# A convolution on rows moved by DMA instead of on transposed features, in a hybrid mixer trunk

## The chip, the cores and the metric

The kernel runs on one core of one Trainium2 chip. The metric is the device time of one launch in microseconds. Of several runs the median counts.

## The reference

One layer of a decoder trunk over 256 tokens of width 2048, in float32: a norm, two causal token mixers fed by one input projection (a gated DeltaNet with 16 heads of 128, and a causal pooling mixer), merged by sigmoid gates and an output projection with a residual; then a gated MLP of width 5632 with a causal depthwise convolution, a residual, and a last norm. What matters here is the path of q, k and v:

```python
proj = jnp.einsum('bsd,de->bse', h, w_in[l])
q, k, v, z, b_raw, a_raw, p_in, g_a, g_b = jnp.split(proj, splits, axis=-1)
qkv = jax.nn.silu(causal_dwconv(jnp.concatenate([q, k, v], axis=-1), conv_qkv_w[l]))
...
def causal_dwconv(x, w):            # width 4 here
    xp = jnp.pad(x, ((0, 0), (width - 1, 0), (0, 0)))
    y = xp[:, 0:seq] * w[0]
    for j in range(1, width):
        y = y + xp[:, j:j + seq] * w[j]
```

Each feature has four taps of its own, and token s sees tokens s−3 to s. After the convolution and silu, q and k are normalised, and the gated delta rule mixes the tokens of each head.

## The kernel before, in words

**Groups.** The mixers run in four groups of four heads (512 features). The loop (L687) does for each group the gemms K, Q, V, P, GB, a short one for the pooling weights, Z and GA. After the four groups come w_out, the MLP's up and down projections and the last norm.

**Weights.** All weights stream in tiles of 512 KB (128 partitions x 1024 float32). For each, `weights()` has a DMA on SyncE's queue fill `raw` (4 buffers), ScalarE rounds it to `whi` (L111), and VectorE forms the remainder `wlo` (L118); `whi` and `wlo` have 3 buffers each, and are made two tiles ahead. In `gemm_a` (L137) a weight tile feeds twelve matmuls: `whi` with the high and the low half of the activations (L148, L149) and `wlo` with the high half (L150). A gemm is eight tiles. Its result stands in PSUM (`psm`, 2 buffers) with tokens on partitions.

**What runs between the matmuls.** At the second tile of a gemm the list `later` is emptied: there the convolution of the gemm before is put. After each weight tile `side()` does one step of `gdn`, the delta rule of the current group, which is a generator: decays (L482 to L511), products of k and q (L518, L520) with their norms, the blocks for a triangular solve sent through DRAM (`cdd`, `lb`, L552 to L556), the solve on VectorE (L563 to L567), its result through DRAM again (`tbd`, `tct`), then `vt`, and from L598 on a chain of small matmuls. `gdn` is started at the second tile of V's gemm. A scheduler places the instructions on the engines' queues within these dependencies; each queue then runs in its order.

**The convolution.** `evict` (L445) copies a gemm's result, scaled by the row norm, from PSUM to `ev` (one buffer, tokens on partitions: 128 x 2 halves x 512 features). `conv_silu` (L452) turns it with eight 128x128 transposes on TensorE (`turned`, L193) so that features lie on partitions and tokens along the row; there a tap is one number per partition, and a shift by s tokens is an offset in the row. Per 128 features ScalarE does the last tap (L463) and VectorE the other three (L466), on `cy` (2 buffers); tanh (L469) and one more VectorE operation (L470) make the silu. For k and q the result with features on partitions is what the delta rule needs. v is needed with tokens on partitions: `gdn` turns it back with eight more transposes (L580) and ScalarE scales it into `vt` (L582).

**The short copies on ScalarE's queue.** All loads that are not weights, `x` or the blocks of the solve go there: norm weights in 16 rows of 512 B (twice), the bias of the MLP's convolution in 44 rows of 512 B (`vrows`), the taps in 96 rows of two times 512 B (`cqrows`) and 66 rows of two times 512 B (`cfrows`), `gwb` in 128 rows of 512 B, `alb` and `dtb` in 128 rows of 64 B each, `psb` four times in 128 rows of 2 KB, later `xt` in 256 rows of 8 KB and `nfin` in 128 rows of 8 KB.

Of the kernel before, what the change touches and what calls it, by code (L numbers as in the profile page):

```python
# [7 lines left out]
F32 = mybir.dt.float32  # L8
F32R = mybir.dt.float32r
I32 = mybir.dt.int32  # L10
AF = mybir.ActivationFunctionType
ALU = mybir.AluOpType

P = 128
S = 256
D = 2048
NH = 16
KD = D // P
# [6 lines left out]
C_Q, C_K, C_V, C_Z = 0, 2048, 4096, 6144  # L25
# [8 lines left out]
def kernel(  # L34
# [20 lines left out]
    nc = tc.nc  # L55
# [11 lines left out]
    def nm(s):  # L67
        cnt[0] += 1
        return f"{s}_{cnt[0]}"

    def pg(shape=(P, 512)):
        return psg.tile(list(shape), F32, tag="g", name=nm("psg"))
# [25 lines left out]
    def weights():  # L98

        begin(taken[0] + AHEAD + 1)  # L100
        taken[0] += 1
        return made[taken[0] - 1]
# [19 lines left out]
    side_work = [iter(())]  # L122

    def side():
        next(side_work[0], None)
# [5 lines left out]
    def pm():  # L131
        return psm.tile([P, 2, 512], F32, tag="m", name=nm("psm"))


    later = []

    def gemm_a(lh, ll, nk):  # L137

        ps = pm()
        for c in range(nk // 2):  # L140
            if c == 1:
                while later:
                    later.pop(0)()
            hi, lo = weights()
            for kk in range(2):
                k = 2 * c + kk
                for t in range(2):
                    mm(ps[:, t, :], lh(k, t), hi[:, kk, :], start=(k == 0), stop=False)  # L148
                    mm(ps[:, t, :], ll(k, t), hi[:, kk, :], start=False, stop=False)  # L149
                    mm(ps[:, t, :], lh(k, t), lo[:, kk, :], start=False, stop=(k == nk - 1))  # L150
                side()
        return ps
# [47 lines left out]
    ident = cpool.tile([P, P], F32, name="ident")  # L200
# [5 lines left out]
    def mtile(i, shape, dt, name):  # L206
        return big.tile(shape, dt, tag=f"m{i}", name=name)

    mix = tc.tile_pool(name="mix", bufs=1)
    mp = mix.__enter__()  # L210
# [17 lines left out]
    for k2 in range(KD // 2):  # L228
# [6 lines left out]
        for kk in range(2):  # L235
# [3 lines left out]
                                           op0=ALU.mult, op1=ALU.subtract)  # L239
# [74 lines left out]
    rs1 = rstd_rows(ssq, None)  # L314
    rsh = cpool.tile([P, 2], F32, name="rsh")
# [110 lines left out]
    for g, win in enumerate(WINDOWS):  # L426
# [3 lines left out]
        for cs in (slice(0, P + PAD), slice(P + PAD, NB)):  # L430
            b = bd[:, cs]
            n = cs.stop - cs.start
# [9 lines left out]
    mhi = []  # L442
    mlo = []

    def evict(ps):  # L445

        e = mp.tile([P, 2, 512], F32, tag="ev", bufs=1, name=nm("ev"))
        for t in range(2):
            nc.scalar.activation(e[:, t, :], ps[:, t, :], AF.Copy, scale=rs1[:, t : t + 1])
        return e  # L450

    def conv_silu(e, kind, g, dst):  # L452

        pts = turned(e)
        y = mp.tile([P, 4, S], F32, tag="cy", bufs=2, name=nm("cy"))
        for f in range(4):
            r = kind * 16 + 4 * g + f
            gs = pts[f // 2][:, f % 2, :]

            def w(j):  # L460
                return cqw[:, j * 48 + r : j * 48 + r + 1]

            nc.scalar.activation(y[:, f, :], gs, AF.Copy, scale=w(3))  # L463
            for j in (2, 1, 0):
                s = 3 - j
                nc.vector.scalar_tensor_tensor(y[:, f, s:], gs[:, : S - s], w(j), y[:, f, s:],  # L466
                                               op0=ALU.mult, op1=ALU.add)
        th = mp.tile([P, 4, S], F32, tag="th", name=nm("th"))
        nc.scalar.activation(th, y, AF.Tanh)  # L469
        nc.vector.scalar_tensor_tensor(dst, th, 1.0, y, op0=ALU.add, op1=ALU.mult)  # L470

    def gdn(g, kq, vT, res):

        ga0 = mp.tile([P, 4, 512], F32, tag="ga0", name=nm("ga0"))
        ga1 = mp.tile([P, 4, 256], F32, tag="ga1", name=nm("ga1"))
        vt = mp.tile([P, 2, 4, P], F32, tag="vt", name=nm("vt"))
        ssk = mp.tile([P, 2, 4], F32, tag="ssk", name=nm("ssk"))
        nk = mp.tile([P, 2, 4], F32, tag="nk", name=nm("nk"))
# [33 lines left out]
        for hp in range(2):  # L512
# [3 lines left out]
            for h in (h0, h0 + 1):  # L516
# [5 lines left out]
                for t, src in ((0, pg0[:, 0:P]), (1, pg1[:, 0, :])):  # L522
                    nc.vector.tensor_tensor_reduce(jk, src, ident, scale=1.0, scalar=0.0, op0=ALU.mult,
                                                   op1=ALU.add, accum_out=ssk[:, t, h : h + 1])
# [6 lines left out]
            for h in (h0, h0 + 1):  # L531
# [4 lines left out]
                                               op0=ALU.mult, op1=ALU.mult)  # L536
# [3 lines left out]
                                               op0=ALU.mult, op1=ALU.mult)  # L540
# [34 lines left out]

        for h in range(4):
            yield
            pvt = pg([P, 2, P])
            for t in range(2):
                nc.tensor.transpose(pvt[:, t, :], vT[:, h, t * P : (t + 1) * P], ident)  # L580
            for t in range(2):
                nc.scalar.activation(vt[:, t, h, :], pvt[:, t, :], AF.Copy, scale=nk[:, t, h : h + 1])  # L582
        for _ in range(WAIT - 3):
            yield
        tcm = mp.tile([P, 8, B0], F32, tag="r1h", name=nm("tcm"))
# [100 lines left out]

    for g in range(4):  # L687
        kq = mp.tile([P, 4, 2, S], F32, tag="kq", bufs=1, name=nm("kq"))
        vT = mp.tile([P, 4, S], F32, tag="vT", bufs=1, name=nm("vT"))
        for kind, dst in ((1, kq[:, :, 0, :]), (0, kq[:, :, 1, :]), (2, vT)):  # L690
            if kind == 2:
                res = []
                later.append(lambda g=g, kq=kq, vT=vT, res=res: side_work.__setitem__(0, gdn(g, kq, vT, res)))
            ps = ps_k0 if kind == 1 and g == 0 else gemm_a(xh, xl, KD)
            e = evict(ps)
            later.append(lambda e=e, kind=kind, g=g, dst=dst: conv_silu(e, kind, g, dst))


        win = WINDOWS[g]
        psb = scales(g)  # L700
        ps = gemm_a(xh, xl, KD)
        e = evict(ps)
        phi = mtile(g, [P, 4, S], F32R, nm("phi"))
        plo = mtile(4 + g, [P, 4, S], F32R, nm("plo"))

        def pooled(e=e, g=g, phi=phi, plo=plo):
            for f2 in range(2):
                pt = pg([P, 2, S])
                for ff in range(2):
                    fs = slice((2 * f2 + ff) * P, (2 * f2 + ff + 1) * P)  # L710
                    mm(pt[:, ff, P:S], e[:, 1, fs], bands[:, g, P + PAD : NB], start=True, stop=False,
                       skip_group_check=True)
                    mm(pt[:, ff, 0 : P + PAD], e[:, 0, fs], bands[:, g, 0 : P + PAD], start=False, stop=True,
                       skip_group_check=True)
                fs = slice(2 * f2, 2 * f2 + 2)
                nc.scalar.copy(phi[:, fs, :], pt)
                nc.vector.tensor_tensor(plo[:, fs, :], pt, phi[:, fs, :].bitcast(F32), op=ALU.subtract)

        later.append(pooled)

        def gate(ps, tag):
            th = mp.tile([P, 2, 512], F32, tag=tag, name=nm("gate"))
            for t in range(2):
                nc.scalar.activation(th[:, t, :], ps[:, t, :], AF.Tanh, scale=rsh[:, t : t + 1])
            return th

        tb = gate(gemm_a(xh, xl, KD), "th")
        ps = gemm_a(lambda k, t: phi[:, k, t * P : (t + 1) * P], lambda k, t: plo[:, k, t * P : (t + 1) * P], 4)
        yb = mp.tile([P, 2, 512], F32, tag="yb", name=nm("yb"))
        nc.vector.tensor_tensor(yb, ps, psb.unsqueeze(1).to_broadcast([P, 2, 512]), op=ALU.mult)  # L730
        nc.vector.scalar_tensor_tensor(yb, tb, 1.0, yb, op0=ALU.add, op1=ALU.mult)

        ps = gemm_a(xh, xl, KD)
        sz = mp.tile([P, 2, 512], F32, tag="sz", name=nm("sz"))
        nc.vector.scalar_tensor_tensor(sz, gate(ps, "th"), 1.0, ps, op0=ALU.add, op1=ALU.mult)
        ta = gate(gemm_a(xh, xl, KD), "th")
        nc.vector.scalar_tensor_tensor(sz, ta, 1.0, sz, op0=ALU.add, op1=ALU.mult)
        sz4 = sz.rearrange("p t (h d) -> p (t h) d", h=4)
        nc.vector.tensor_tensor(sz4, sz4, gwb.unsqueeze(1).to_broadcast([P, 8, P]), op=ALU.mult)
        drain()  # L740
        nc.vector.tensor_tensor(sz, res[0].rearrange("p t h d -> p t (h d)"), sz, op=ALU.mult)
        nc.vector.tensor_tensor(sz, sz, yb, op=ALU.add)
        mh = mtile(g, [P, 4, S], F32R, f"mhi{g}")
        ml = mtile(4 + g, [P, 4, S], F32R, f"mlo{g}")
        mhi.append(mh)
        mlo.append(ml)

        def mixed(sz=sz, mh=mh, ml=ml):
            for f2, pt in enumerate(turned(sz)):
                fs = slice(2 * f2, 2 * f2 + 2)  # L750
                nc.scalar.copy(mh[:, fs, :], pt)
                nc.vector.tensor_tensor(ml[:, fs, :], pt, mh[:, fs, :].bitcast(F32), op=ALU.subtract)

        later.append(mixed)
# [14 lines left out]
    for c in range(4):  # L769
        ps = gemm_a(at(mhi), at(mlo), KD)  # L770
# [5 lines left out]
        for k2 in range(2):  # L776
# [5 lines left out]
            for kk in range(2):  # L782
# [4 lines left out]
                                               op0=ALU.mult, op1=ALU.subtract)  # L787
# [9 lines left out]
    for c in range(DFF // 512):  # L797
        ps = gemm_b(lambda k: fhl[:, k], KD)
# [13 lines left out]
        ps = gemm_b(lambda k: fhl[:, k], KD)  # L812
# [15 lines left out]
    for c in range(2):  # L828
        ps = pm()
# [18 lines left out]
    for t in range(2):  # L848
# [14 lines left out]
        for c in (0, 2, 1, 3):  # L863
            xs = xt[:, t, c * 512 : (c + 1) * 512]
            if c < 2:
                nc.vector.scalar_tensor_tensor(xs, xs, rs, nfin[:, c * 512 : (c + 1) * 512],
                                               op0=ALU.mult, op1=ALU.mult)
# [34 lines left out]
```

## Time and profile before

| | |
|---|---|
| median of 3 runs | 1593.93 us (1593.29 to 1594.85) |
| the profiled execution | 1594.1 us, span 1592.3 us |
| TensorE busy | 1568.1 us, 98% |
| VectorE busy | 1066.7 us, 67% |
| ScalarE busy | 750.1 us, 47% |
| GpSimd busy | 115.7 us, 7% |
| DMA | 291.62 MB, 183 GB/s over the span |

In the profile PE is TensorE's matmul side, PEld its weight loads, DVE VectorE, ACT ScalarE, POOL GpSimd, SP SyncE. A group's row reads: line, engine, operation, output <- inputs, shapes, count | busy time, mean ns of one | idle time of the engine just before, and what ended most of it. A matmul's own time there (0.39 us) is longer than the pace at which matmuls follow each other, because they overlap. In the chain of waits a row is start, length, what; in the timeline it is start, length, engine, line, operation, with the idle time before it in brackets. A row of the issues view gives queue, count, KB of each and the median time from issue to landing. Line numbers in the text are those of the kernel before, except where the new code is meant.

### The profile page before, as it was taken

The numbers are of one execution on the slowest core, as the hardware profiler recorded it, in microseconds if no ns is written. First come the engines' busy times: TensorE is split into PE (matmuls) and PEld (weight loads), VectorE is DVE, ScalarE is ACT, GpSimd is POOL, SyncE is SP. The second block draws the span as 40 slices with busy tenths as digits, with TensorE's granted clock in tenths as the row PEclk, the third lists the DMA queues.
The fourth block names the chain that finished last, engine by engine and source line by source line (L and its number), as shares of the span: only waits on it lengthen the run. The fifth ranks groups of instructions, "written<-read, shape, count | busy, mean of one in ns | idle before, by whom it ended". The sixth has DMA issues, their size and how long they took to land.

```text
span 1592.3 us, 21435 instructions
## 1 busy us (share of the span) xinstructions
PE 1568.1 (98%) x8116; PEld 1317.5 (83%) x8116; DVE 1066.7 (67%) x1624; ACT 750.1 (47%) x969; POOL 115.7 (7%) x132
## 2 busy tenths in 40 slices
PE   8999999999999999999999999999999999999997
PEld 6878888888888888887788888888888888888886
DVE  6778758786778757786555777666666677444445
ACT  6455435544455445544454544444444444333334
POOL 3020100110020100102000000000000000000000
PEclk9999999999999999999999999999999999999999
DMA  7656656566556656665556666666666666656563
GB/s 251 185 153 191 193 144 179 168 189 176 159 152 189 198 145 177 170 191 162 200 184 182 187 187 192 190 186 187 185 195 186 187 191 209 201 191 197 191 193 132
DMA packets 159789, 291.62 MB, mean 183 GB/s; under 512 B 17974, under 2 KB 21062, under 8 KB 159302
## 3 DMA queue, kind: packets, MB, share of 16 engines
q1 hardware_dynamic: 157792, 285.77, 60.8%
q10 hardware_dynamic: 1894, 4.48, 0.8%
q8 instruction: 63, 1.03, 0.3%
q14 instruction: 40, 0.33, 0.1%
HBM read 287.07 MB, written 3.15 MB: 182 GB/s over the span
## 4 chain that ended last, share of the span: by engine, by line
PE 89%; DVE 3%; DMA 3%; issue 3%; POOL 2%; SPq 1%; ACT 0%; DVEq 0%; POOLq 0%
PE psm L150 12%; PE psm L149 12%; PE psm L148 12%; PE psm L172 10%; PE psg L172 10%; PE psg L173 5%; PE psm L173 5%; PE psg L836 3%; PE psg L838 3%; PE psg L837 3%; PE psm L838 2%; PE psm L836 2%; PE psm L837 2%; DVE wlo L118 1%; PE psg L518 1%
## 5 line engine op out<-in xcount | busy, mean ns | idle before, releaser
L118 DVE TENSOR_TENSOR wlo<-raw,whi 128x1024 fp32r<-128x1024 f32 x528 | 657.8, 1247 | 414.1 <-ACT whi L111 407.8
L111 ACT CAST whi<-raw 128x1024 fp32r<-128x1024 f32 x530 | 557.8, 1053 | 753.7 <-PE psm L149 331.4
L150 PE MATMUL psm<-wlo,xhl 128*128 128x512 f32 x896 | 352.9, 394 | 2.7 <-DVE wlo L118 2.7
L148 PE MATMUL psm<-whi,xhl 128*128 128x512 f32 x896 | 352.1, 393 | 1.9 <-ACT xhl L237 1.9
L149 PE MATMUL psm<-whi,xhl 128*128 128x512 f32 x896 | 351.9, 393 | 0.0
L172 PE MATMUL psm<-fhl,whi 128*128 128x512 f32 x704 | 245.9, 396 | 0.0
L172 PE MATMUL psg<-fhl,whi 128*128 128x512 f32 x704 | 237.8, 394 | 0.0
L150 PEld LDWEIGHTS psm<-wlo,xhl 128*128 128x128 f32 x896 | 168.6, 188 | 38.4 <-DVE wlo L118 4.3
L148 PEld LDWEIGHTS psm<-whi,xhl 128*128 128x128 f32 x896 | 168.7, 188 | 35.9 <-ACT xhl L237 2.3
L149 PEld LDWEIGHTS psm<-whi,xhl 128*128 128x128 f32 x896 | 168.6, 188 | 34.7
L173 PE MATMUL psm<-fhl,wlo 128*128 128x256 f32 x704 | 194.2, 279 | 0.0
L173 PE MATMUL psg<-fhl,wlo 128*128 128x256 f32 x704 | 178.6, 279 | 0.0
L172 PEld LDWEIGHTS psm<-fhl,whi 128*128 128x128 f32 x704 | 131.3, 188 | 30.4
L172 PEld LDWEIGHTS psg<-fhl,whi 128*128 128x128 f32 x704 | 129.2, 188 | 24.0
L173 PEld LDWEIGHTS psg<-fhl,wlo 128*128 128x128 f32 x704 | 132.4, 188 | 6.9
L173 PEld LDWEIGHTS psm<-fhl,wlo 128*128 128x128 f32 x704 | 132.5, 188 | 1.1
L836 PE MATMUL psg<-whi,hhi 128*128 128x512 f32 x176 | 68.6, 390 | 0.0
L836 PE MATMUL psm<-whi,hhi 128*128 128x512 f32 x176 | 68.5, 389 | 0.0
L837 PE MATMUL psm<-whi,hlo 128*128 128x512 f32 x176 | 68.5, 389 | 0.0
L837 PE MATMUL psg<-whi,hlo 128*128 128x512 f32 x176 | 68.5, 389 | 0.0
L838 PE MATMUL psm<-wlo,hhi 128*128 128x512 f32 x176 | 68.5, 389 | 0.0
L838 PE MATMUL psg<-wlo,hhi 128*128 128x512 f32 x176 | 61.7, 389 | 0.0
(233 smaller groups left out, 1515.3 us busy)
## 6 DMA issues: line engine op xcount, KB each, us to landing
raw<-in_w_in_dram SPq DMA_DIRECT2D x226, 512.0 KB, 3.8
raw<-in_w_up_dram SPq DMA_DIRECT2D x176, 512.0 KB, 3.9
raw<-in_w_down_dram SPq DMA_DIRECT2D x88, 512.0 KB, 3.9
raw<-in_w_out_dram SPq DMA_DIRECT2D x32, 512.0 KB, 3.6
raw<-in_pool_w_dram SPq DMA_DIRECT2D x8, 512.0 KB, 3.9
x<-in_x_dram SPq DMA_DIRECT2D x4, 512.0 KB, 8.5
lb<-cdd SPq DMA_DIRECT2D x16, 128.0 KB, 2.7
xt<-in_x_dram ACTq DMA_DIRECT2D x1, 2048.0 KB, 8.3
```

Source lines behind the costliest of these rows:

```text
L111: nc.scalar.copy(hi, raw)
L118: nc.vector.tensor_tensor(lo, raw, hi.bitcast(F32), op=ALU.subtract)
L148: mm(ps[:, t, :], lh(k, t), hi[:, kk, :], start=(k == 0), stop=False)
L149: mm(ps[:, t, :], ll(k, t), hi[:, kk, :], start=False, stop=False)
L150: mm(ps[:, t, :], lh(k, t), lo[:, kk, :], start=False, stop=(k == nk - 1))
L172: mm(ps[f], hi[:, kk, fs], rhl(k), start=(k == 0), stop=False, skip_group_check=True)
L173: mm(ps[f][:, 1, :], lo[:, kk, fs], rhl(k)[:, 0, :], start=False, stop=(k == nk - 1), skip_group_check=True)
L518: mm(pg0, kq[:, h, 0, 0:P], kq[:, h, :, :], start=True, stop=True)
L836: mm(acc[c][t], lh(k, t), hi[:, kk, :], start=(k == 0), stop=False)
L837: mm(acc[c][t], ll(k, t), hi[:, kk, :], start=False, stop=False)
L838: mm(acc[c][t], lh(k, t), lo[:, kk, :], start=False, stop=(k == KF - 1))
```

## The change

For v, `conv_silu` is no longer called. V's gemm is evicted with half the row norm (`rsh`). Then, on tokens:

- Three tiles get copies of `ev` moved on by one, two and three tokens. For a move by j, rows 0 to 127−j of `ev` (each 4 KB, both token halves side by side) go to rows j to 127; the last j rows of the first half (2 KB each) go to the first j rows of the second half; GpSimd clears the first j rows of the first half. The copies are issued from ScalarE's queue. The first two tiles use the two buffers of `cy`, the third has one of its own.
- The four taps, 512 numbers each, are loaded over all 128 partitions by four copies of 256 KB on SyncE's queue, into the buffers of `sz` and `yb`.
- Four products and three sums of 128x1024 on VectorE, tanh on ScalarE and one VectorE operation give v with tokens on partitions. `vt` is scaled from it directly; the transposes at L580 are gone.

The copies are issued right behind the eviction; the arithmetic goes on the list `later`, at the second tile of P's gemm. In the new order of VectorE's queue the product on the first move stands behind `wlo` of P's third weight tile, ahead of the end of Q's convolution and of `wlo` of P's fourth tile; in the first group ahead of `wlo` of P's fourth tile too, behind part of the side work.

```diff
-    def evict(ps):
+    def evict(ps, by=None):
+        by = rs1 if by is None else by
         e = mp.tile([P, 2, 512], F32, tag="ev", bufs=1, name=nm("ev"))
         for t in range(2):
-            nc.scalar.activation(e[:, t, :], ps[:, t, :], AF.Copy, scale=rs1[:, t : t + 1])
+            nc.scalar.activation(e[:, t, :], ps[:, t, :], AF.Copy, scale=by[:, t : t + 1])
         return e
+
+    def later_tokens(e, g):
+        moved = []
+        for j in (1, 2, 3):
+            m = mp.tile([P, 2, 512], F32, name=nm("mv"), **(dict(tag="cy", bufs=2) if j < 3 else dict(tag="mv")))
+            nc.gpsimd.memset(m[0:j, 0, :], 0.0)
+            nc.scalar.dma_start(m[j:P], e[0 : P - j])
+            nc.scalar.dma_start(m[0:j, 1, :], e[P - j : P, 0, :])
+            moved.append(m)
+        taps = []
+        for n, tag in enumerate(("sz", "yb")):
+            tp = mp.tile([P, 2, 512], F32, tag=tag, name=nm("taps"))
+            for i in range(2):
+                nc.sync.dma_start(tp[:, i, :], conv_qkv_w[0, 2 * n + i, C_V + 512 * g : C_V + 512 * g + 512]
+                                  .partition_broadcast(P))
+                taps.append(tp[:, i, :].unsqueeze(1).to_broadcast([P, 2, 512]))
+        return moved, taps
+
+    def conv_tokens(e, moved, taps):
+        m1, m2, m3 = moved
+        for m, j in ((m1, 2), (m2, 1)):
+            nc.vector.tensor_tensor(m, m, taps[j], op=ALU.mult)
+        nc.vector.tensor_tensor(m1, m1, m2, op=ALU.add)
+        for m, j in ((e, 3), (m3, 0)):
+            nc.vector.tensor_tensor(m, m, taps[j], op=ALU.mult)
+            nc.vector.tensor_tensor(m1, m1, m, op=ALU.add)
+        th = mp.tile([P, 2, 512], F32, tag="th", name=nm("th"))
+        nc.scalar.activation(th, m1, AF.Tanh)
+        nc.vector.scalar_tensor_tensor(m1, th, 1.0, m1, op0=ALU.add, op1=ALU.mult)
+        return m1
...
-    def gdn(g, kq, vT, res):
+    def gdn(g, kq, vals, res):
...
-            pvt = pg([P, 2, P])
             for t in range(2):
-                nc.tensor.transpose(pvt[:, t, :], vT[:, h, t * P : (t + 1) * P], ident)
-            for t in range(2):
-                nc.scalar.activation(vt[:, t, h, :], pvt[:, t, :], AF.Copy, scale=nk[:, t, h : h + 1])
+                nc.scalar.activation(vt[:, t, h, :], vals[0][:, t, h * P : (h + 1) * P], AF.Copy,
+                                     scale=nk[:, t, h : h + 1])
...
-        vT = mp.tile([P, 4, S], F32, tag="vT", bufs=1, name=nm("vT"))
-        for kind, dst in ((1, kq[:, :, 0, :]), (0, kq[:, :, 1, :]), (2, vT)):
-            if kind == 2:
-                res = []
-                later.append(lambda g=g, kq=kq, vT=vT, res=res: side_work.__setitem__(0, gdn(g, kq, vT, res)))
+        for kind, dst in ((1, kq[:, :, 0, :]), (0, kq[:, :, 1, :])):
             ps = ps_k0 if kind == 1 and g == 0 else gemm_a(xh, xl, KD)
             e = evict(ps)
             later.append(lambda e=e, kind=kind, g=g, dst=dst: conv_silu(e, kind, g, dst))
+        res = []
+        vals = []
+        later.append(lambda g=g, kq=kq, vals=vals, res=res: side_work.__setitem__(0, gdn(g, kq, vals, res)))
+        e = evict(gemm_a(xh, xl, KD), rsh)
+        mt = later_tokens(e, g)
+        later.append(lambda e=e, mt=mt, vals=vals: vals.append(conv_tokens(e, *mt)))
```

## The prediction

> **What bounds the kernel now.** I read the page first (engines, queues, chain, groups), then the windows, the forms of each line, the issues, and the timeline around the first group's V and P gemms.
>
> ```profile
> span 1592.3 us, 21435 instructions
> ...
> PE 1568.1 (98%) x8116; PEld 1317.5 (83%) x8116; DVE 1066.7 (67%) x1624; ACT 750.1 (47%) x969; POOL 115.7 (7%) x132
> ...
> q1 hardware_dynamic: 157792, 285.77, 60.8%
> q10 hardware_dynamic: 1894, 4.48, 0.8%
> ...
> PE 89%; DVE 3%; DMA 3%; issue 3%; POOL 2%; SPq 1%; ACT 0%; DVEq 0%; POOLq 0%
> ...
> L118 DVE TENSOR_TENSOR wlo<-raw,whi 128x1024 fp32r<-128x1024 f32 x528 | 657.8, 1247 | 414.1 <-ACT whi L111 407.8
> ...
> L150 PE MATMUL psm<-wlo,xhl 128*128 128x512 f32 x896 | 352.9, 394 | 2.7 <-DVE wlo L118 2.7
> ```
>
> TensorE is busy 98% of the span and carries 89% of the chain. The kernel is bound by its matmuls: a TensorE instruction removed is a gain of its own length, and anything added elsewhere costs only what it makes TensorE wait. The one way by which VectorE reaches TensorE is `wlo`: a weight tile's twelve matmuls need it, and over 896 matmuls they waited 2.7 us in all. The whole execution took 1594.1 us, 1.8 us more than its span and 0.2 us above the median of the three runs (1593.93), so sums against it and against the median are the same within their error.
>
> How long can VectorE be held up before TensorE notices? Before, it is held up once per group by the copy that fills `lb`. VectorE's timeline in group 0, then TensorE's:
>
> ```profile
> 127.84 0.42 DVE L565 TENSOR_TENSOR tmp<-lb,tb 128x248 f32<-128x248 f32 x1 [3.86 <-DMA lb<-cdd]
> ...
> 128.95 1.22 DVE L118 TENSOR_TENSOR wlo<-raw,whi 128x1024 fp32r<-128x1024 f32 x1
> ```
> ```profile
> 130.22 0.50 PE L150 MATMUL psm<-wlo,xhl 128*128 128x512 f32 x1 [0.93 <-DVE wlo L118]
> ```
>
> A hold of 3.86 us cost TensorE 0.93 us: a stall of a few microseconds is hidden by the `wlo` tiles made ahead (three buffers), and beyond that each microsecond is passed on in full.
>
> **The change part by part.** Prices first, from the view of groups by form:
>
> ```profile
> L466 DVE SCALAR_TENSOR_TENSOR cy<-psg,cqw,cy 128x254 f32<-128x254 f32 x48 | 21.3, 472 | 0.0
> ...
> L449 ACT ACTIVATE ev<-psm,rs 128x512 f32<-128x512 f32 x32 | 20.2, 681 | 1.6 <-PE psm L150 1.6
> L813 DVE TENSOR_TENSOR gs<-gs,y 128x1024 f32<-128x1024 f32 x11 | 13.5, 1226 | 1.1
> L193 PE MATMUL psg<-ident,ev 128*128 128x128 f32 x96 | 12.8, 272 | 0.0
> ```
> ```profile
> 67.55 0.92 PE psg L193 x8
> ```
>
> *Transposes removed.* Eight of v at L193 and eight back at L580 per group, 64 in all. In the chain eight take 0.92 us, so 64 × 0.115 = 7.4 us come off TensorE. That is the whole gain.
>
> *Arithmetic swapped.* Per group VectorE loses 12 operations at 0.47 (5.7 us) and gets seven of 128x1024 at 1.23 (8.6 us): 3 us more on an engine at 67%, free by itself. ScalarE loses four copies at L463, the `vt` copies only read elsewhere; GpSimd gets three memsets of one to three rows (7% busy). All at nothing.
>
> *The moves.* Six copies per group are issued from ScalarE's queue: 127, 126 and 125 rows of 4 KB moved on by one, two and three tokens, and three wraps of one to three rows. No row shows an SBUF-to-SBUF copy or one of 127 rows, so its price must be bounded. How copies are divided over the 16 engines can be read off this queue, q10:
>
> ```profile
> raw<-in_w_in_dram SPq DMA_DIRECT2D x226, 512.0 KB, 3.8
> ...
> xt<-in_x_dram ACTq DMA_DIRECT2D x1, 2048.0 KB, 8.3
> ...
> cfrows<-in_conv_ffn_w_dram ACTq DMA_DIRECT2D x1, 66.0 KB
> ...
> vrows<-in_conv_ffn_b_dram ACTq DMA_DIRECT2D x1, 22.0 KB
> ...
> dtb<-in_dt_bias_dram ACTq DMA_DIRECT2D x1, 8.0 KB
> ```
>
> Fourteen copies go through it, between `xt` and `dtb` in that list. By their shapes in the code they have 1680 rows: 528 of 512 B, 256 of 64 B, 512 of 2 KB, 384 of 8 KB. The queue counts 1894 packets, 214 more. One closing packet per engine used would be 14 × 16 = 224 if every copy ran on all 16; ten are missing. Only two copies have row counts that 16 doesn't divide: `vrows` of the bias with 44 rows, `cfrows` with 66. If each ran on 11 engines (44 = 11 × 4, 66 = 11 × 6), the sum is 12 × 16 + 22 = 214, exactly. Had they been cut into blocks of rows rounded up, they would use 15 and 14, and three would be missing. So a copy uses the largest number of engines up to 16 that divides its rows. 127 is prime: the first move runs on one engine; 126 rows run on 14; 125 on 5. The Trainium skill, page "DMA: Bandwidth & Descriptors", section "Why a DMA increments its semaphore by 16 and not by 1", states this division and names 127 partitions as a case that gets one engine; no run of before shows that case.
>
> What one engine moves, from the busiest stretch of the windows view (columns: length, busy of PE, PEld, DVE, ACT, POOL, clock, DMA share, GB/s):
>
> ```profile
> 12.00:18.00 6.00, 6.00 (x24) 5.02 (x23) 5.76 (x13) 5.57 (x15) 0.00 (x0) 1.00 0.88 318
> ```
>
> 318 / (0.88 × 16) = 22.6 GB/s per engine, so 127 × 4096 B = 0.520 MB take 23.0 us. By q1's row (60.8% of 16 engines for 1592.3 us over 285.77 MB = 54.2 us per MB) they take 28.2. I take 23.0, a queue full of packets being nearer to that stretch, and allow 18 to 29. The skill's page just named, section "Specifications", gives some 27 GiB/s per engine, which would make an estimate of 18 us and a sum 20 us lower.
>
> *When the move is late.* Let E be the end of group g's V gemm. The eviction takes 2 × 0.68 = 1.4 us, then ScalarE has two small exponentials and the wrap's issue: the long move is issued near E + 2.4. A raw tile lands 3.8 us after issue although its 32 KB per engine take 1.45 at 22.6 GB/s, so some 2.35 us come on top; and the same engine carries its sixteenth of what else flies: 1 MB of taps (2.9 us) and one or two raw tiles (1.45 each), much of it before, so 2 (0 to 6). Landing: E + 2.4 + 23.0 + 2.35 + 2 = E + 29.8. In the changed kernel's order VectorE has the product on the first move (L475) right behind `wlo` of P's third weight tile, and waits there. Queued behind it are the last operation of Q's convolution (L503), then `wlo` of P's fourth tile: 3 × 1.2 = 3.6 us, so that tile is ready at E + 33.4. TensorE has three tiles and two matmuls of the fourth, 38 × 0.23 = 8.7 us (its pace is in the rows below), and nothing else: the side work waits for Q's convolution too. Stall: 33.4 − 8.7 = **24.7 us per group**. The cover of a few microseconds is in that number already.
>
> The second move reuses the buffer that L503 frees, so it is issued after the first has landed: 9 rows per engine (1.6 us) + 2.35 against some 3.6 us of VectorE work on what lies between; I take 1 us per group (0 to 2). The third, 125 rows on five engines, lies behind the first on the shared engine (25 rows, 4.5 us) and VectorE reaches it 4.8 us later: nothing. Moves: 4 × 25.7 = **103 us**, with ends 4 × 18 = 72 (transfer 18, no shared traffic, nothing for the second move) and 4 × 36 = 144 (transfer 29, traffic 6, second move 2).
>
> *The clock after a stall.* The chain in the start-up, after a first idle time:
>
> ```profile
> 12.82 0.43 PE psm L149
> ...
> 14.81 0.23 PE psm L148
> ```
>
> TensorE's matmuls took 0.43 us at 12.8 and 0.23 at 14.8; a stretch of some 4 us at half pace would cost 2 us. I put that behind each long stall: 4 × 2 = 8 (0 to 10).
>
> *The tail of the mixers.* The heads' side work starts some seven weight tiles later, so the last group's closes inside w_out, whose first two tiles then hold weight buffers. Waits of that kind are there already:
>
> ```profile
> 773.16 0.50 PE L148 MATMUL psm<-whi,mhi 128*128 128x512 f32 x1 [0.91 <-ACT whi L111]
> ...
> 774.42 0.50 PE L150 MATMUL psm<-wlo,mhi 128*128 128x512 f32 x1 [0.53 <-DVE wlo L118]
> ```
>
> One tile costs 1.4 us; four more such, half covered by side matmuls, +3 (0 to 8). *Taps:* four 256 KB copies per group on SyncE's queue, 4 MB over the kernel at a DMA share of 0.6: hidden, except 0.5 us in the start-up, where they stand ahead of raw tiles.
>
> **Sum**: 1594.1 − 7.4 + 103 + 8 + 3 + 0.5 = **1701 us**. Its own range: 1594 − 7 + 72 + 0 = 1659 to 1594 − 7 + 144 + 10 + 8 = 1749.
>
> **The rivals.**
> *The moves are spread over all engines, and still late.* Against: the 214 packets. For: no 127-row copy is shown. Then a move costs what a raw tile does, 3.8 us, + 2 of shared traffic, and lands at E + 8.2; `wlo` at E + 11.8 against 8.7 and 1 for the second move give 4 us of stall per group, with the tail 1594 − 7 + 16 + 3 = 1606.
> *Spread and hidden: the change is faster.* The point that decides is E + 8.7 − 3.6 = E + 5.1: a first move that lands by then costs nothing. With the issue straight behind the eviction (E + 1.4) and 3.8 us it lands at E + 5.2. Then only transposes and tail count: 1594 − 7 + 3 = 1590, at best 1587.
> *One engine, slower still.* Reading and writing SBUF through one engine might cost both ways (46 us), or raw tiles take half of it: + 23 us per group, 1701 + 92 = 1793. For: no row shows SBUF to SBUF. Against: raw tiles stop flowing once TensorE stalls.
>
> **How the numbers follow.** One engine at the price above 0.83; spread and late 0.06; spread and hidden 0.05; slower still 0.06. What a measurement tells from no change is about 0.2%, 3.2 us. Faster: 0.04, most of the hidden case. Same: 0.03, the rest of it and the mildest of the late one. Slower: 0.93. The range runs from 1640 (the low end, less 5 us per group for an engine quicker still) to 1749 and leaves out all three rivals and little else, some 0.2.
>
> **What would show it.** Right: in the waits, VectorE at L475 on the copy from `ev` four times at some 20 us or more; the issues view gives the long move 25 to 31 us to land, the 126-row one a few; TensorE's wait for `wlo` of L118 at L150 grows from 2.7 to about 100 us, in four pieces, each behind a V gemm, with matmuls at 0.43 us behind each; L193 drops from 96 to 64 transposes of `ev`, L580 is gone. Wrong: a long move that lands within 6 us; a VectorE wait at L475 without a stall of TensorE; or a time under 1610.

## The result, and the profile after

The changed kernel takes 1677.39 us in the median of its runs (1677.33 to 1681.23) against 1593.93; the ratio is 1.0528, with an interval of 1.0516 to 1.0540. It is slower by 83 us, where 1701 was forecast, with a range of 1640 to 1749. The profiled execution is the longest of the runs: its span is 1679.1 us, 86.8 more than before.

The page of the changed kernel:

```profile
span 1679.1 us, 21338 instructions
...
PE 1578.3 (94%) x8052; PEld 1318.2 (79%) x8052; DVE 1079.4 (64%) x1604; ACT 746.0 (44%) x953; POOL 125.6 (7%) x144
...
q10 hardware_dynamic: 3654, 10.72, 1.8%
...
L148 PE MATMUL psm<-whi,xhl 128*128 128x512 f32 x896 | 355.7, 397 | 40.3 <-ACT whi L111 38.6
L150 PE MATMUL psm<-wlo,xhl 128*128 128x512 f32 x896 | 355.1, 396 | 12.6 <-DVE wlo L118 12.6
...
L475 DVE TENSOR_TENSOR mv<-mv,taps 128x1024 f32<-128x1024 f32 x8 | 9.8, 1225 | 93.9 <-DMA mv<-ev 71.6
```

TensorE is busy 10.2 us longer and idle 76.6 us longer (100.8 against 24.2). VectorE stands idle 93.9 us ahead of the products at L475. Its waits and TensorE's (waited for: total, times, longest):

```profile
PE psm L148 <- ACT whi L111: 40.9, 7, 10.4
PE psg L551 <- DVE kq L503: 26.3, 3, 9.0
PE psm L150 <- DVE wlo L118: 13.1, 8, 9.1
```

So TensorE waits on two things, and the first is ScalarE's cast, not `wlo`. The timeline of group 1 shows why (V's gemm ends near 293.0). ScalarE and its queue first, then TensorE, then VectorE:

```profile
295.94 10.01 ACTq L459 DMA_DIRECT2D mv<-ev  x1
306.28 3.44 ACTq L460 DMA_DIRECT2D mv<-ev  x1
309.77 1.06 ACT L502 ACTIVATE th<-cy 128x1024 f32<-128x1024 f32 x1 [13.46 <-issue]
310.73 1.98 ACT L111 CAST whi<-raw 128x1024 fp32r<-128x1024 f32 x2
```
```profile
311.81 0.79 PE L148 MATMUL psm<-whi,xhl 128*128 128x512 f32 x1 [9.58 <-ACT whi L111]
322.07 2.08 PE L551 MATMUL psg<-kq 128*128 128x512 f32 x2 [9.04 <-DVE kq L503]
```
```profile
319.65 1.23 DVE L475 TENSOR_TENSOR mv<-mv,taps 128x1024 f32<-128x1024 f32 x1 [22.31 <-DMA mv<-ev]
320.79 1.22 DVE L503 SCALAR_TENSOR_TENSOR kq<-th,cy 128x1024 f32<-128x1024 f32 x1
```

The long move was issued at 295.2 (0.66 us). The next issue, of the third move, takes ScalarE's queue 10.0 us, its wrap 3.4 more, and the casts behind them come at 310.7. Meanwhile VectorE waits for the long move until 319.65, 24.4 us after its issue (24.4 to 25.5 in the four groups). TensorE's two gaps, 9.6 and 9.0 us, are one stall with few matmuls in it; in the four groups the stall is 17.6 to 19.2 us, 74 in all.

What the DMA engines did in that time, first the windows view (length, busy of PE, PEld, DVE, ACT, POOL, clock, DMA share, GB/s), then the queues in the same window (packets, MB, share of 16 engines):

```profile
314.00:322.00 8.00, 0.00 (x0) 0.00 (x0) 2.35 (x3) 0.00 (x0) 0.00 (x0) 0.50 0.06 27
```
```profile
q10 hardware_dynamic: 53, 0.21, 6.5%
```

One engine of 16 is 6.25%. For eight microseconds it alone works, at 27 GB/s, and the fifteen others stand idle with everything else.

### The profile page after: what moved, and what is told of

Same layout as the page of the kernel before. It is cut to its first block, busy times and chain, and to the rows that moved or that the text cites. A ratio compares the mean times of both kernels' runs of the same rounds, so it can differ in the third digit from the quotient of the medians.

```text
span 1679.1 us, 21338 instructions
## 1 busy us (share of the span) xinstructions
PE 1578.3 (94%) x8052; PEld 1318.2 (79%) x8052; DVE 1079.4 (64%) x1604; ACT 746.0 (44%) x953; POOL 125.6 (7%) x144
## 4 chain that ended last, share of the span: by engine, by line
PE 54%; DMA 2%; POOL 1%; DVE 0%; issue 0%; ACT 0%; SPq 0%; DVEq 0%; POOLq 0%
PE psm L172 10%; PE psg L172 10%; PE psg L173 5%; PE psm L173 5%; PE psm L150 3%; PE psm L148 3%; PE psm L149 3%; PE psg L869 2%; PE psg L871 2%; PE psg L870 2%; PE psm L870 2%; PE psm L871 2%; PE psm L869 2%; DMA mv<-ev 1%; PE psg L551 0%
## 5 line engine op out<-in xcount | busy, mean ns | idle before, releaser
L148 PE MATMUL psm<-whi,xhl 128*128 128x512 f32 x896 | 355.7, 397 | 40.3 <-ACT whi L111 38.6
L150 PE MATMUL psm<-wlo,xhl 128*128 128x512 f32 x896 | 355.1, 396 | 12.6 <-DVE wlo L118 12.6
L475 DVE TENSOR_TENSOR mv<-mv,taps 128x1024 f32<-128x1024 f32 x8 | 9.8, 1225 | 93.9 <-DMA mv<-ev 71.6
```

Source lines behind the costliest of these rows:

```text
L475: nc.vector.tensor_tensor(m, m, taps[j], op=ALU.mult)
```

## The experiments

**The division of rows.** The first run cuts every move at 112 rows, which 16 divides.

```diff
-            nc.scalar.dma_start(m[j:P], e[0 : P - j])
+            nc.scalar.dma_start(m[j : j + 112], e[0:112])
+            nc.scalar.dma_start(m[j + 112 : P], e[112 : P - j])
```

> Each move is cut into two copies: its first 112 rows (16 x 7) and the remaining 15, 14 or 13; nothing else is changed, and the order on VectorE's queue around the products stays the one of the changed kernel. Theory (the 127 rows of the first move lie on one engine, 127 x 0.16 us of packets): the first move lands some 4 us after its issue instead of 24, the issue of the third move no longer takes 10 us of ScalarE, the stall behind each V gemm falls from 19 us to 1 to 3, and the time to 1594 - 7 + 8 + 7 (tail as in the changed kernel) + 1 = about 1603 us (1596 to 1608). Rival 1 (copies from SBUF to SBUF are slow by themselves, or these 1.5 MB collide with the weight tiles): the bytes are the same, so the landing stays over 12 us and the time over 1640. Rival 2 (it is the longer arithmetic on VectorE that starves TensorE): no change, 1675.

Measured: 1603.08 us, ratio to before 1.0054 (1.0039 to 1.0069). The same bytes, two copies for one, and 74 us are gone. VectorE's wait for the moves and TensorE's for `wlo` in that run:

```profile
DVE mv L476 <- DMA mv<-ev: 22.5, 7, 5.2
...
PE psm L150 <- DVE wlo L118: 9.9, 9, 3.2
```

The wait at the product falls from 22 to 24 us to 5 at most, and the stalls behind the V gemms to 1.2 to 3.7 us per group, where 1 to 3 were expected. Copies from SBUF to SBUF are not slow by themselves, and the longer arithmetic starves nobody.

**No moves at all.** The products read `ev` in place of the moved tiles:

```diff
-            nc.vector.tensor_tensor(m, m, taps[j], op=ALU.mult)
+            nc.vector.tensor_tensor(m, e, taps[j], op=ALU.mult)
```

> Leaves the moves out: the three tiles are written by the products straight from ev, without the copies and the clearing of their first rows; taps, seven VectorE operations, tanh and the rest stay. Theory: what is left is the removed transposes (-7.4 us), the taps, the arithmetic and the later tail: 1588 to 1596, no wait of VectorE for a copy of ev, no stall of TensorE over 1 us behind a V gemm. Rival 2 (arithmetic on VectorE starves TensorE): stalls behind the V gemms of some microseconds remain and the time is over 1600.

Measured: 1589.06 us, ratio 0.9967 (0.9954 to 0.9980). This is what the rest of the change is worth: some 5 us faster. From one V eviction to the next the groups take 182.0 us in the mean against 184.8 before; behind the last V, up to the MLP, 208.0 against 204.7, so the later closing part takes some of it back.

**A ladder of row counts.** The second and third moves are cut as above; the first differs from group to group.

```diff
+            cut = (P - j, 122, 124, 112)[g] if j == 1 else 112
+            nc.scalar.dma_start(m[j : j + cut], e[0:cut])
```

> A ladder in one kernel. The second and third moves are cut at 112 rows as in the spread version; the first move has one copy of 127 rows in group 0, 122 + 5 rows in group 1, 124 + 3 in group 2 and 112 + 15 in group 3. If a copy uses the largest number of engines up to 16 that divides its rows, these are 1, 2, 4 and 16 engines with 127, 61, 31 and 7 rows of 4 KB each, at 0.16 us a row 20, 10, 5 and 1 us. VectorE's waits at the product on the first move then come down in steps of 10, 5 and 4 us from one group to the next, and TensorE's stalls are near 18, 8, 3 and 1 us: some 30 us in all, 1624 us. Rival (the third move's issue, which holds ScalarE's queue for 10 us, is the cause): since that one is cut here, group 0 already shows a stall under 10 us. Rival (a copy of over 112 rows runs on all 16 engines, cut by bytes): no steps between the groups.

Measured: 1640.06 us in one run. VectorE's timeline at the product on the first move, groups 0 to 3 (127, 122, 124, 112 rows):

```profile
117.80 1.23 DVE L478 TENSOR_TENSOR mv<-mv,taps 128x1024 f32<-128x1024 f32 x1 [23.11 <-DMA mv<-ev]
...
313.04 1.23 DVE L478 TENSOR_TENSOR mv<-mv,taps 128x1024 f32<-128x1024 f32 x1 [11.96 <-DMA mv<-ev]
...
505.38 1.22 DVE L478 TENSOR_TENSOR mv<-mv,taps 128x1024 f32<-128x1024 f32 x1 [10.08 <-DMA mv<-ev]
...
690.33 1.23 DVE L478 TENSOR_TENSOR mv<-mv,taps 128x1024 f32<-128x1024 f32 x1 [4.53 <-DMA mv<-ev]
```

124 rows wait less than 122, so it isn't the bytes. In group 1's stall the windows view shows two engines' share:

```profile
306.00:312.00 6.00, 0.00 (x0) 0.00 (x0) 0.00 (x0) 0.00 (x0) 0.00 (x0) 0.78 0.13 53
```

0.13 is two sixteenths and 53 GB/s twice the 27 of above. The steps are 11, 2 and 6 us where 10, 5 and 4 were expected, and the whole is 16 us above the expectation. TensorE's stalls are 17.5, 10.6, 6.9 and 3.3 us where 18, 8, 3 and 1 were expected. In group 2 the third move's pieces, issued next on the same queue, run on the four engines too, which may be why it waits so long there. Only the first and the last step are as the rule has them; the middle one is too small. Group 0's stall is 17.5 us with the third move cut (17.6 with it whole), and its issue still takes 9.9 us: the hold comes from the long copy ahead of it in the queue, not from the odd row count of the one behind. Behind 122 rows the same issue takes 0.6 us, behind 124 2.0.

**Another queue.** All six copies keep their rows and are issued by GpSimd.

```diff
-            nc.scalar.dma_start(m[j:P], e[0 : P - j])
+            nc.gpsimd.dma_start(m[j:P], e[0 : P - j])
```

> The six copies of each group keep their rows and are issued from GpSimd's queue instead of ScalarE's. This frees ScalarE of the issues, and puts the product on the first move behind P's fifth weight tile on VectorE's queue, so some 5 us more are covered. Theory with the same division of rows on this queue: the move still lands 22 us or more after its issue, some 12 us of stall are left per group, 1594 - 7 + 48 + 6 + 8 = about 1650 us. If this queue cuts a copy into blocks of rows over all 16 engines, the move lands within some 6 us and the time is near 1592 to 1602.

Measured: 1588.64 us, ratio 0.9965 (0.9951 to 0.9979), a third of a per cent faster than the kernel before. The issues view, and the queues while the moves of group 0 run (95 to 99 us):

```profile
mv<-ev POOLq DMA_DIRECT2D x4, 508.0 KB, 5.5
```
```profile
q0 software_dynamic: 281, 1.00, 99.3%
```

127 rows land in 5.5 us and the queue fills all 16 engines. So GpSimd's queue divides rows in another way than ScalarE's. The Trainium skill, page "DMA: Bandwidth & Descriptors", section "Why a DMA increments its semaphore by 16 and not by 1", names this exception, blocks of rows rounded up over 16 engines for some direct copies issued there; the run agrees.

**Nobody waits: is the long move free then?** The next run keeps the moves as in the changed kernel and puts the products a gemm later, by making the cleared rows depend on P's result.

```diff
-            nc.gpsimd.memset(m[0:j, 0, :], 0.0)
...
+        for j, m in zip((1, 2, 3), mt[0]):
+            nc.gpsimd.tensor_scalar(m[0:j, 0, :], e[0:j, 0, :], 0.0, None, op0=ALU.mult)
+        later.append(held)
```

> The moves stay as in the changed kernel: one copy of 127 rows, ScalarE's queue. But nobody waits for them early: the clearing of the first rows is made to depend on P's eviction (zero times P's values, same result), so VectorE's products stand behind GB's fourth weight tile, some 32 us after the V gemm's end, and Q's tanh stands ahead of the moves on ScalarE's queue. (V's evicted tile lies in another buffer for this, and the delta rule's values come ten tiles later.) Theory: the long transfer itself costs nothing, no wait of VectorE for a copy of ev over 1 us; what is left is the third move's issue, which still holds ScalarE's queue for 10 us, with the casts of P's fourth tile behind it: a stall of 9 to 12 us per group through whi instead of wlo, 1594 - 7 + 44 + 6 (clock) + 10 (tail) = 1647 us (1630 to 1665). Rival (holding ScalarE's queue is harmless, only the wait for the first move matters): 1605 us or less. Rival (one engine's traffic slows the weight tiles): stalls through raw tiles, 1660 and more.

Measured: 1681.55 us, a miss. Its timeline has the hold (ScalarE, then TensorE), and a wait that had been left in:

```profile
308.30 0.38 ACT L536 ACTIVATE dec<-psg 128x256 f32<-128x256 f32 x1 [10.01 <-issue]
```
```profile
315.44 0.79 PE L148 MATMUL psm<-whi,xhl 128*128 128x512 f32 x1 [4.60 <-ACT whi L111]
```
```profile
331.84 1.23 DVE L477 TENSOR_TENSOR ev<-ev,taps 128x1024 f32<-128x1024 f32 x1 [12.71 <-DMA mv<-ev]
```

The product of `ev` with its own tap overwrites `ev`, so it must stand until the copies have read it, and it had stayed early. One wait for the copy had gone, and the next one on the same copy took its place. The run beside it is the same with the moves cut at 112 rows:

> The same as the late version, with each move cut at 112 rows as in the spread version, so neither the landing nor the issue takes long; nine issues of 0.6 to 1.3 us remain on ScalarE's queue. Theory: the stalls behind the V gemms of the spread version (1.4 to 4 us each) were the wait for landing on VectorE; with the late products they go, and the groups take 182 us from V to V as without moves: 1591 to 1601 us, the spread being the tail, which starts still later here. Rival (nine issues on ScalarE delay the casts): stalls through whi of 1 to 3 us per group stay, 1600 to 1608.

Measured: 1595.32 us, ratio 1.0008 (0.9998 to 1.0018). No stall above 1 us is left behind the V gemms, and the groups take 182 to 184 us: the stalls of the spread version were the landing, and nine issues on ScalarE's queue cost next to nothing (182.8 us per group on average, 182.0 without moves).

Then the overwriting product was given a tile of its own:

```diff
-        for m, j in ((e, 3), (m3, 0)):
-            nc.vector.tensor_tensor(m, m, taps[j], op=ALU.mult)
+        for m, j, d in ((e, 3, pe), (m3, 0, m3)):
+            nc.vector.tensor_tensor(d, m, taps[j], op=ALU.mult)
```

> The late version again, with the wait that was left in it taken out: there the product of ev with its own tap was written over ev, and so had to stand until all copies had read it (VectorE idle 12.7 us at that line). Here it goes to a tile of its own. All moves stay in one copy each on ScalarE's queue. Theory: nobody waits for the long move any more; the hold of ScalarE's queue by the third move's issue stays, with the casts behind it: a stall of about 9 us per group through whi and none through wlo, groups of some 193 us from V to V instead of 203, 1594 - 7 + 36 + 6 + 10 = 1639 us (1625 to 1650). Rival (the transfer's 127 rows on one engine cost in themselves, wherever the wait is): stalls near 18 us per group, 1675.

Measured: 1643.92 us, ratio 1.0319 (1.0289 to 1.0349), where 1639 was expected: behind the V gemms TensorE now stalls 7.2 to 8.4 us per group, all of it on ScalarE behind the held queue: in group 0 for the cast, in the others for a decay (L537, 2.7 to 3.5 us) and then for the cast (3.8 to 4.7). Is the hold then the price? With only the first move left on that queue:

> As the run beside it, with only the first move (127 rows, one copy, one engine) left on ScalarE's queue, and the second and third issued from GpSimd's. So nothing stands behind the long copy in its queue, and nobody waits for it for 32 us. Theory: the one-engine transfer of over 20 us is hidden whole: no stall over 1 us behind a V gemm, 182 us from V to V, 1590 to 1600 us (the tail is later here than in the GpSimd version). Rival (one engine's traffic slows the weight tiles or the other moves): 1605 us and more, with casts waiting for raw tiles.

Measured: 1643.40 us, ratio 1.0316. This miss is the most telling one. ScalarE's queue is free, nobody waits for 32 us, and the loss is the same. Waits of TensorE, ScalarE and VectorE, then the queues from 313 to 319 us, in group 1:

```profile
PE psm L150 <- DVE wlo L118: 38.1, 9, 7.0
...
ACT whi L111 <- DMA raw<-in_w_in_dram: 77.1, 27, 4.2
...
DVE mv L475 <- DMA mv<-ev: 28.7, 4, 7.6
DVE tmp L599 <- DMA lb<-cdd: 18.2, 4, 5.5
```
```profile
q10 hardware_dynamic: 26, 0.11, 4.3%
q1 hardware_dynamic: 25, 0.05, 2.1%
```

Together 6.4%: the one engine again, now taking a 4 KB row of the move and a 2 KB packet of a weight tile in turn, 26 of one and 25 of the other. A weight tile is complete only when its part on that engine is; the casts wait for raw tiles 77.1 us in all (2.2 before). The move itself, issued at 284.9, is waited for until 322.1: 37 us instead of 24, as the weight tiles no longer stand still. So the wait for the move is back: TensorE's own waits here are for `wlo`, twice per group, first behind VectorE's wait for the move (6.5 to 7.6 us) and then behind its wait for `lb`, with casts late as well. This run alone doesn't show what the crowded engine costs when nobody waits at all.

The Trainium skill, on the page named above, section "Queues, rings and completion order", has each engine go round the queues that it has work for, draining a packet of typically some 9 to 17 descriptors from one before it switches. That it goes round agrees with the counts; the size doesn't: in the trace the starts alternate row by row.

**The cost by itself.** The kernel before, with one useless copy per group added:

```diff
+                m = mp.tile([P, 2, 512], F32, tag="sz", name=nm("mv"))
+                nc.scalar.dma_start(m[1:128], e[0:127])
```

> The disputed cost by itself. The kernel before (v turned and turned back as ever), with one useless copy added per group: 127 rows of V's evicted result to a tile that nobody reads, in one copy on ScalarE's queue, nothing behind it in that queue. No engine waits for it. New theory, from the run with only the first move left on ScalarE's queue: there the one engine took a 4 KB row and a 2 KB packet of a weight tile in turn (0.159 + 0.084 us), so a weight tile, with 16 packets on each engine, needed 3.9 us or more instead of the 2.72 at which TensorE uses them, over some 31 us; that costs 8 to 12 us per group with nobody waiting for the copy: 1594 + 40 = 1634 us (1625 to 1645), casts waiting for raw tiles by some 60 to 80 us in all. Older theory (a copy that nobody waits for is free): 1594 to 1597.

> The same with 112 rows in the useless copy, 88% of the bytes, on all 16 engines by the division of rows. New theory: landed within some 5 us, no more than one weight tile late by 1 to 2 us, hidden by the raw tiles ahead: 1593 to 1597 us. Rival (it is the added bytes or the issue, not the one engine): 88% of the other's loss.

Measured: 1640.89 us with 127 rows, ratio 1.0294 (1.0264 to 1.0324), and 1594.31 with 112, ratio 0.9999 (0.9987 to 1.0010). With 88% of the bytes, nothing is left of the loss. The time is inside the expectation, but not by the path that it named: casts waited for raw tiles only 22.9 us. What waited was the solve, and TensorE for the `wlo` queued behind it (run with 127 rows, then before):

```profile
DVE tmp L565 <- DMA lb<-cdd: 48.0, 4, 13.5
...
PE psm L150 <- DVE wlo L118: 39.5, 8, 11.7
```
```profile
DVE tmp L565 <- DMA lb<-cdd: 12.7, 4, 3.9
```
```profile
303.54 0.37 SPq L553 DMA_DIRECT2D cdd<-cd  x1
304.87 3.46 SPq L109 DMA_DIRECT2D raw<-in_w_in_dram  x1
317.56 1.73 SPq L556 DMA_DIRECT2D lb<-cdd  x4
```

In SyncE's timeline the copies for `lb` are issued 14 us after that of `cdd`, which they wait for (4.4 us before, 293.76 to 298.11). `cdd` goes out in many small packets, and on the shared engine each takes its turn with a 4 KB row, as the queues from 313 to 316 us show:

```profile
q10 hardware_dynamic: 18, 0.07, 6.0%
q1 hardware_dynamic: 18, 0.00, 0.5%
```

Behind `lb` the weight tiles queue. Of the 46.8 us by which this span is longer than before, 35.3 are idle time of TensorE and 11.5 are longer busy time.

**An earlier start of the delta rule**, on the version with GpSimd's queue:

> The version with the moves on GpSimd's queue, with the delta rule's steps started two weight tiles earlier (at the last tile but one of Q's gemm: the decays need neither q nor k). If the closing part after the last group (some 4 us longer than before in the GpSimd version) hangs on the start of these steps, it shrinks by 1 to 4 us, to 1585 to 1588. If it hangs on Q's convolution, which stays where it was, nothing changes: 1588.6.

Measured: 1597.18 us, ratio 1.0021 (1.0012 to 1.0030): slower, against both expectations. The closing part didn't shrink (207.1 us from the last V eviction to the MLP, 206.5 with GpSimd's queue alone, 204.7 before); the groups take 184.6 us from V to V instead of 182.0. The start reordered all queues; what the closing part hangs on stays open. The fastest version seen is the one with the moves on GpSimd's queue.

## Why the prediction was right, point by point

*The bound.* Right: TensorE set the time, and what VectorE or ScalarE was held up came through once the tiles made ahead were used up. Group 1's stall began 9.2 us behind E, where 8.7 was put: 36 matmuls and about 1 us of side work instead of 38 matmuls, so that the numbers agree is partly luck. One step was wrong: `wlo` is not the one way by which VectorE reaches TensorE. It also does so through `kq`, and ScalarE through its casts. Of TensorE's waits in the changed kernel `wlo` has 12.6 us, where about 100 was named as the sign; the casts have 38.6, and L551 waited 26.3 for `kq`.

*The division of rows, read from 214 packets of the kernel before.* Right, and it decided. The run with 112 rows, the ladder and the window with one sixteenth show it. The two rivals that spread the moves, one of which saw the change faster, fell with it.

*The transfer.* 27.35 us (23.0 + 2.35 + 2) was put from issue to landing; 24.4 to 25.5 were measured. The rate was the mis-sized term: the engine moved 27 GB/s, not 22.6, so 19 us for the rows. The Trainium skill's figure (page "DMA: Bandwidth & Descriptors", section "Specifications") of some 27 GiB/s, which is 29 GB/s, was the nearer one; it was set aside for the row of the start-up.

*The stall.* 24.7 us per group was put, with 1 more for the second move; 17.6 to 19.2 were measured, 74 in all instead of 103. In group 1 the stall is 6.1 us shorter. 3.2 of them are the earlier landing. 1.7 come from matmuls that the sum didn't have or had elsewhere: side work ahead of the stall (0.5 us net) and two matmuls within it (1.2). The last 1.2 come from a step that was wrong: "nothing else: the side work waits for Q's convolution too". It does, but it comes ahead of `wlo`: in three of the four groups TensorE restarted on L551, in group 1 at 322.07, straight behind L503, and `wlo` of P's fourth tile was made during it. (By its own terms the upper end is 36.7 us per group, 147 and 1752, where 36, 144 and 1749 stand.)

*The issues.* Costed at under a microsecond each; the third move's took 10 us. The prediction had nothing on a queue that is held. Here it lay within the longer wait for the landing. Where that wait is gone, the hold stalls TensorE by 7 to 8 us per group (the run with the own tile); where the hold is gone as well (only the first move left on that queue), the time is the same.

*The clock.* Right in kind, half in size: 8 us was put. TensorE was busy 1578.3 us, in the run without moves, which has the same matmuls, 1562.3: 16 us were lost to the slower pace. Each stall restarts twice, and the pairs at L551 took 2.08 us where the same pairs took 1.02 before (L518). The granted clock behind group 1's stall:

```profile
322.00:329.00 7.00, 6.93 (x16) 4.27 (x17) 6.41 (x9) 1.05 (x1) 1.34 (x2) 0.64 0.76 226
```

*Transposes and tail.* Put at −7.4 and +3; the run without moves has both together at −5. From the last V eviction to the MLP the changed kernel takes 28.6 us more, the other groups 19.1 more on average from V to V: 9.5 us remain, above the range of 0 to 8 if they are put down to the tail. But the run without moves has 6.1 of them too (its closing part is 3.3 us longer than before, as forecast, its groups 2.8 shorter). No run separates the other 3.

*The sum.* The stalls came out 29 us shorter than put and the slower pace 8 us longer. That the total is off by only 24 us, 1677 for 1701, is partly these two errors against each other.

*The rival "one engine, slower still".* Its mechanism, that raw tiles take part of the engine, was dismissed because they stop flowing once TensorE stalls. That is what happens in the changed kernel; where TensorE goes on, the shared engine made the move take 37 us, and in the run with the useless copy, for which nobody waits, it cost 47 us.

## What to carry to other kernels

Before moving rows by DMA, look at the row count: a copy of 127 rows by ScalarE's queue ran on one engine and took 24 us; cut into 112 + 15 rows it had landed within 6 to 8, and from GpSimd's queue in 5.5. A copy that crowds one engine wasn't hidden by having nobody wait for it, since other copies needed that engine for their own sixteenth. When a wait is taken out, look for the next instruction that waits on the same thing, an overwrite as well as a read.

## What the runs showed of the hardware that was not expected

Issuing a copy isn't always short: behind a 127-row copy in the same queue the next issue took 9.6 to 10.4 us, against 0.6 behind one of 122 rows, and the engine that issues is held for that time with all its work. That room in the one engine's queue is what is short there is a guess; no run measures it.

One crowded engine out of 16, crowded four times for 26 to 29 us, cost 47 us (1640.89 against 1594.03) with the DMA engines at a mean share of 0.6: the mean says nothing of the fullest one.
